# Holding back the last pair's second half in the recurrent layer's closing weave

## The chip, the cores and the metric

The kernel runs on one core of a Trainium2 chip. The metric is the device time of one execution in microseconds (us). Three executions of the kernel before the change took 1380.64, 1379.71 and 1378.60 us; the median is 1379.71 us. One further execution was recorded by the profiler, and every duration below comes from that one.

## The reference

A two-layer encoder trunk works on one sequence of 512 positions with 1024 channels. Layer 0 mixes positions with a recurrence of 12 heads (of 64 channels each) and, beside it, with attention of 4 heads into 256 memory tokens. Layer 1 uses chunked attention in place of the recurrence. Each layer ends in an output projection and a gated channel mixer. Cut to what the change touches, layer 0 is:

```
h = rms_norm(x, ln1[0]);  p = h @ a_w_in[0]
mix = rwkv7_time_mix(h, p[..., :3 * D_MIX], ...)        # the recurrence, 12 heads
mo  = memory_attention(p[..., 3 * D_MIX:], mem_n, ...)  # softmax(q k^T / 8) v, 4 heads
x = x + jnp.concatenate([mix, mo], axis=-1) @ w_out[0]

# inside rwkv7_time_mix, per head:
def step(state, inp):
    r_t, w_t, k_t, v_t, a_t, b_t = inp
    sa = jnp.einsum('bhvk,bhk->bhv', state, a_t)
    state = (state * w_t[:, :, None, :] + sa[..., None] * b_t[:, :, None, :]
             + v_t[..., None] * k_t[:, :, None, :])
    return state, jnp.einsum('bhvk,bhk->bhv', state, r_t)
# then a norm over each head's 64 channels, a bonus term, and a gate g
```

## The kernel before, in words

Everything is kept transposed, channels on the 128 partitions and the 512 positions along the free axis. A product of two fp32 operands is done as three products of a high and a low part (`r1h` and `r1l` of an activation, `whi` and `wlo` of a weight tile): `dense` writes them as pairs of matmuls on L198 and L199 for `whi`, then those on L202 for `wlo`.

The 12 heads of the recurrence go in 6 pairs, 0 to 5, and each pair goes through three generators of steps. `prepare` projects r, k and v, forms the keys, and solves a triangular system per 64-position chunk: the vector engine (DVE) works through 31 dependent rows in tile `Xs` (L661 to L668), the result goes to DRAM as `d2` and comes back as `Tt` (L671 and L674, issued on SP's queue). `front` forms products of keys and queries (`ML`, `VT`). `back` is the second half of a pair. It loads the gate's weights `g2` (L771), transposes a part of `Tt` (L775), does a chain of small matmuls (L780, L788, L794, L804, L815, L821, L830, with copies and vector operations between), then steps a state through the 8 chunks (L835 on the tensor engine PE, L836 on DVE, and the output on L840), normalises (copy L844, square L847, reduction L549, reciprocal root, transposes L558, then L856 to L858), applies the gate (L184 to L186, L867) and writes the pair's rows of `r1h` and `r1l` (L214, L215).

The order of the work is set when the program is built. `weave` takes several generators with a weight each. It keeps a clock of its own in ns, always takes a step from the one that is least far along for its weight, and adds the cost that the step yields. A step that yields `(cost, wait)` also keeps its generator from going on until the weave's clock has moved on by `wait`; a step that yields a condition keeps it until the condition holds. The tile framework then schedules the recorded instructions and gives every engine a fixed queue, worked off strictly in its order.

The last weave of layer 0 has four generators: the `back` of pair 4 (`a_`); `front` and then `back` of pair 5 (`b_`), which uses other buffers (`other_tiles`) and waits, just before its gate, for pair 4's `back` to be over; the memory's queries, reload of pairs 0 to 3 and memory attention (`q_mem`, `flush_mix`, `mA`); and `ahead`, the first two output tiles of the output projection for all inputs but pair 5's. In memory attention a score tile (L921) goes through a row maximum (L269), two exponentials (L273), a reciprocal (L275), two scalings (L278), four transposes each into two banks (L286), copies (L289) and the product with the values (L296). The small PSUM tiles `pss` of all four generators share a pool of 4 banks.

After the weave, `out_proj` finishes these two tiles with pair 5's rows and goes on with six more. The residual input `xT` (L951) is loaded into memory that the recurrent layer occupied until then.

## Time and profile before

| | |
|---|---|
| time of the profiled execution | 1377.77 us |
| its span, first to last instruction | 1376.0 us |
| median of the three timed executions | 1379.71 us |
| PE busy | 1319.7 us, 96% of the span |
| DVE busy | 826.9 us, 60% |
| scalar engine (ACT) busy | 611.6 us, 44% |
| mean granted TensorE clock | 0.987 of full speed |
| the last weave of layer 0 | about 290 to 379 us in the span |

PE is busy nearly all the time, so the profile is read by its exceptions: stretches in which PE waits, and stretches in which its clock is granted at less than full speed. A row of the timeline gives start, duration, engine, line, operation, the tiles as out<-in, and how many instructions were merged; in square brackets stands how long the engine had been idle before and who released it. In the trace one matmul of 64 or 128 columns between fp32 tiles counts twice (x32 where the program's order has x16).

### The profile page before, as it was taken

How to read it: one execution, taken by the hardware profiler on the slowest of the kernel's cores; microseconds unless marked ns; L12 is line 12 of the kernel's file. 1: busy time of each engine (PE TensorE's matmuls, PEld its weight loads, DVE VectorE, ACT ScalarE, POOL GpSimd, SP SyncE). 2: the span in 40 equal slices, each digit the busy share in tenths (PEclk: the TensorE clock that was granted, in tenths of full speed). 3: DMA queues.
4: the chain of work that ended last, by engine and by line, in shares of the span. 5: the costliest groups of instructions: out<-in, count | busy, mean ns of one | idle time of the engine just before them, and what ended most of it. 6: DMA issues, size and time to landing. Idle time of an engine off the chain costs nothing. (4 is left out here: it accounts for less than half of the span.)

```text
span 1376.0 us, 20868 instructions
## 1 busy us (share of the span) xinstructions
PE 1319.7 (96%) x8266; PEld 1071.2 (78%) x8266; DVE 826.9 (60%) x1752; ACT 611.6 (44%) x1022; POOL 34.1 (2%) x55
## 2 busy tenths in 40 slices
PE   6999999995999999999999999999999999999996
PEld 5777777774688888888888878786788888888886
DVE  7876789774666555565333667657665565563324
ACT  5556555552444333333222566657443333332321
POOL 3000000000000000000000000000000000000000
PEclk9999999997999999999999999999999999999998
DMA  5276544451042223223232422223223222222332
GB/s 181 83 208 136 109 108 110 99 142 42 24 146 92 92 94 106 92 93 102 84 98 85 152 91 74 90 92 99 93 92 103 96 93 102 98 88 85 104 94 75
DMA packets 63506, 139.18 MB, mean 101 GB/s; under 512 B 24624, under 2 KB 28336, under 8 KB 63408
## 3 DMA queue, kind: packets, MB, share of 16 engines
q1 hardware_dynamic: 60672, 127.89, 29.3%
q0 software_dynamic: 2736, 9.96, 4.2%
q8 instruction: 65, 1.06, 0.3%
q14 instruction: 33, 0.27, 0.1%
HBM read 131.01 MB, written 6.82 MB: 100 GB/s over the span
## 5 line engine op out<-in xcount | busy, mean ns | idle before, releaser
L175 DVE TENSOR_TENSOR wlo<-wraw,whi 128x1024 fp32r<-128x1024 f32 x183 | 218.9, 1197 | 128.4 <-PE psd L202 118.3
L169 ACT CAST whi<-wraw 128x1024 fp32r<-128x1024 f32 (+1 forms) x202 | 207.6, 1029 | 153.3 <-PE psd L199 38.5
L198 PE MATMUL psd<-r1h,whi 128*128 128x512 f32 x336 | 136.6, 407 | 1.3 <-ACT whi L169 1.2
L198 PE MATMUL psf<-r2h,whi 128*128 128x512 f32 x352 | 137.2, 390 | 0.0
L198 PE MATMUL psf<-r1h,whi 128*128 128x512 f32 x352 | 137.2, 390 | 0.0
L199 PE MATMUL psf<-r1l,whi 128*128 128x512 f32 x352 | 137.1, 390 | 0.0
L199 PE MATMUL psf<-r2l,whi 128*128 128x512 f32 x352 | 137.1, 390 | 0.0
L199 PE MATMUL psd<-r1l,whi 128*128 128x512 f32 x336 | 134.1, 399 | 0.0
L202 PE MATMUL psd<-r1h,wlo 128*128 128x512 f32 x336 | 92.5, 403 | 3.1 <-DMA wlo<-in_wA_dram 3.1
L199 PE MATMUL psd<-f3l,whi 128*128 128x512 f32 (+1 forms) x238 | 88.7, 377 | 0.0
L198 PE MATMUL psd<-f3h,whi 128*128 128x512 f32 (+1 forms) x238 | 88.6, 377 | 0.0
L358 DVE TENSOR_TENSOR tmp<-psf,rho 128x512 f32<-128x512 f32 x44 | 30.4, 692 | 94.7 <-PE psf L202 94.7
L202 PE MATMUL psf<-r1h,wlo 128*128 128x512 f32 x352 | 87.0, 389 | 0.0
L202 PE MATMUL psf<-r2h,wlo 128*128 128x512 f32 x352 | 86.9, 389 | 0.0
L198 PE MATMUL psd<-r2h,whi 128*128 128x512 f32 (+1 forms) x200 | 77.6, 392 | 0.1
L198 PEld LDWEIGHTS psd<-r1h,whi 128*128 128x128 f32 x336 | 63.8, 190 | 17.4 <-issue 2.4
L199 PE MATMUL psd<-r2l,whi 128*128 128x512 f32 (+1 forms) x200 | 76.4, 385 | 0.8 <-DVE r2l L215 0.8
L202 PEld LDWEIGHTS psf<-r1h,wlo 128*128 128x128 f32 x352 | 66.1, 188 | 13.7
L202 PEld LDWEIGHTS psf<-r2h,wlo 128*128 128x128 f32 x352 | 66.1, 188 | 13.7
L199 PEld LDWEIGHTS psf<-r1l,whi 128*128 128x128 f32 x352 | 66.1, 188 | 13.6
L198 PEld LDWEIGHTS psf<-r2h,whi 128*128 128x128 f32 x352 | 66.1, 188 | 13.7
L199 PEld LDWEIGHTS psf<-r2l,whi 128*128 128x128 f32 x352 | 66.1, 188 | 13.6
(352 smaller groups left out, 2429.2 us busy)
## 6 DMA issues: line engine op xcount, KB each, us to landing
wraw<-in_ffn_in_dram SPq DMA_DIRECT2D x88, 512.0 KB, 3.3
wraw<-in_ffn_out_dram SPq DMA_DIRECT2D x32, 448.0 KB, 3.3
wraw<-in_wA_dram SPq DMA_DIRECT2D x20, 512.0 KB, 4.3
wlo<-in_wA_dram POOLq DMA_DIRECT2D x17, 512.0 KB, 7.7
wraw<-in_w_out_dram SPq DMA_DIRECT2D x16, 512.0 KB, 3.8
wraw<-in_ffn_out_dram SPq DMA_DIRECT2D x16, 512.0 KB, 4.1
wraw<-in_wB_dram SPq DMA_DIRECT2D x8, 512.0 KB, 3.4
Lr<-d SPq DMA_DIRECT2D x24, 128.0 KB, 5.5
```

The source lines that it names most:

```text
L169: SC.copy(hi[:, :n], raw)
L175: V.tensor_tensor(lo[:, :n], raw, hi[:, :n], op=ALU.subtract)
L198: PE.matmul(ps, wh[:, j * P:(j + 1) * P], ah, start=start and n == 0, stop=False)
L199: PE.matmul(ps, wh[:, j * P:(j + 1) * P], al, start=False, stop=False)
L202: PE.matmul(ps, wl[:, j * P:(j + 1) * P], act(k)[0], start=False, stop=stop and n == len(ks) - 1)
L358: V.tensor_tensor(v[:], pv[:], rho[:], op=ALU.mult)
```

## The change

A new generator `later` yields one step of cost 0 and a wait of the given number of ns of the weave's clock. It is put between `front` and `back` of pair 5 with 25000 ns, so that `back` of pair 5 takes its first step only when the weave's clock has gone 25 us further. No instruction is added to or taken from the program on any engine; the queues' order changes.

```diff
+    def later(ns):
+        yield 0, ns
+
     AHEAD = [0, 1, 2, 3, 4, 6, 7]
     a_, b_ = NPAIR - 2, NPAIR - 1
     weave([(told(back(a_, Ts[a_], dst_mix), "back"), 1.5 * BACK_COST),
-           (chain(front(b_, Ts[b_]), back(b_, Ts[b_], dst_mix, other_tiles, lambda: "back" in over)),
+           (chain(front(b_, Ts[b_]), later(25000), back(b_, Ts[b_], dst_mix, other_tiles, lambda: "back" in over)),
             1.5 * (FRONT_COST + BACK_COST)),
```

What it moves shows at three places. The first is PE's queue before the change, after the second of the memory's query projections (`psd` on L202). `AR` on L780 is pair 5's transposed `Tt`, `ML` with `W` or `Tt_93` belongs to pair 4, `Tt_94` to pair 5, and `kmT` with `kn` is memory attention.

```order
L202 MATMUL psd<-r1h,wlo 128x512 x6
L830 MATMUL psl<-ML,VT 64x64 x8
L202 MATMUL psd<-r1h,wlo 128x512 x2
L780 MATMUL pss<-AR,ML 32x32
L788 MATMUL pss<-VT,ML 64x64 x12
L780 MATMUL pss<-AR,ML 32x32 x15
L788 MATMUL pss<-VT,ML 64x64 x4
L804 MATMUL pss<-VT,Tt_93 64x128 x8
L794 MATMUL pss<-Tt_94,AR 32x32 x16
```

The same place in the changed kernel's PE queue:

```order
L821 MATMUL pss<-VT,ML 64x64 x16
L198 MATMUL psd<-r1h,whi 128x512
L199 MATMUL psd<-r1l,whi 128x512
L202 MATMUL psd<-r1h,wlo 128x512 x6
L830 MATMUL psl<-ML,VT 64x64 x16
L202 MATMUL psd<-r1h,wlo 128x512 x2
L921 MATMUL pss<-kmT_85,kn 128x256 x4
L835 MATMUL psl<-W,MQ 64x64 x2
L840 MATMUL psl<-MQ,W 64x64 x2
L921 MATMUL pss<-kmT_85,kn 128x256 x4
```

Pair 5's L780 no longer follows the projection; pair 4's chain has moved ahead of it (L804, L815 and L821 stand between the projection's matmuls), and memory attention and pair 4's state steps come next.

The second place is further on in the changed kernel's PE queue, where pair 5's second half now begins. `tmp` on L549 and L558 belongs to pair 4's norm, and `kh` to the last scores of memory attention.

```order
L186 MATMUL psl<-gsh,g2l 128x512
L549 MATMUL pss<-cst,tmp 128x2 x4
L921 MATMUL pss<-kmT_85,kh 128x256 x4
L780 MATMUL pss<-AR,ML 32x32 x16
L788 MATMUL pss<-VT,ML 64x64 x16
L794 MATMUL pss<-Tt_94,AR 32x32
L184 MATMUL psl<-gsh,Xs 128x512
```

L780 of pair 5 has moved behind pair 4's state and norm and behind all eight score tiles of memory attention.

The third place is the end of the weave on PE. Before the change it reads as follows, where `psd_4632` and `psd_4661` are the output projection's first two tiles:

```order
L202 MATMUL psd_4632<-r1h_68,wlo_4628 128x512 x7
L199 MATMUL psd_4661<-r1l_69,whi_4656 128x512
L198 MATMUL psd_4661<-r1h_68,whi_4656 128x512
L199 MATMUL psd_4661<-r1l_69,whi_4656 128x512
L202 MATMUL psd_4661<-r1h_68,wlo_4657 128x512 x7
L198 MATMUL psd_4632<-r1h_68,whi_4627 128x512
L199 MATMUL psd_4632<-r1l_69,whi_4627 128x512
L202 MATMUL psd_4632<-r1h_68,wlo_4628 128x512
```

In the changed kernel these two tiles are `psd_4596` and `psd_4625`, `psd_4729` is the third, and `pss_4667` takes the transposes of pair 5's norm:

```order
L202 MATMUL psd_4625<-r1h_68,wlo_4621 128x512 x6
L558 MATMUL pss_4667<-cst_66,tmp_4665 128x128 x4
L202 MATMUL psd_4625<-r1h_68,wlo_4621 128x512
L198 MATMUL psd_4596<-r1h_68,whi_4591 128x512
L199 MATMUL psd_4596<-r1l_69,whi_4591 128x512
L202 MATMUL psd_4596<-r1h_68,wlo_4592 128x512
L198 MATMUL psd_4625<-r1h_68,whi_4620 128x512
L199 MATMUL psd_4625<-r1l_69,whi_4620 128x512
L202 MATMUL psd_4625<-r1h_68,wlo_4621 128x512
L198 MATMUL psd_4729<-r1h_68,whi_4725 128x512
```

Before, the transposes of pair 5's norm stand some forty matmuls ahead of the first that needs pair 5's rows; now only one L202 is left between them. From the third tile of the output projection on, both programs have the same order on PE.

## The prediction

> **What bounds the kernel now.** I read the page first. Its second part cuts the span into 40 slices of 34.4 us; a digit is the busy share in tenths, and PEclk the granted clock.

> ```profile
> span 1376.0 us, 20868 instructions
> ...
> PE   6999999995999999999999999999999999999996
> ...
> PEclk9999999997999999999999999999999999999998
> ```

> PE bounds the kernel everywhere but in the tenth slice (309.6 to 344 us), where it is half busy at a lower clock. That slice lies in the closing weave. Next I cut this stretch by stages; the columns are the stage, its length, then busy time on PE, PEld, DVE, ACT and POOL, granted clock and DMA.

> ```profile
> 311.70:326.40 14.70, 0.02 (x1) 0.05 (x2) 8.60 (x29) 0.81 (x2) 0.00 (x0) 0.57 0.33 75
> 326.40:340.90 14.50, 14.33 (x289) 12.95 (x289) 4.15 (x10) 5.28 (x15) 0.00 (x0) 0.84 0.03 5
> 340.90:361.70 20.80, 20.80 (x207) 13.71 (x206) 13.12 (x47) 11.11 (x34) 0.00 (x0) 1.00 0.01 2
> 361.70:380.40 18.70, 18.47 (x90) 13.91 (x89) 11.68 (x34) 8.18 (x19) 0.00 (x0) 1.00 0.24 85
> ```

> PE does nothing for 14.7 us, then is busy without a break. The timeline says who releases it, and what is done by when (PE, DVE, then SP's queue):

> ```profile
> 303.84 1.09 PE L804 MATMUL pss<-VT,Tt 64*64 64x128 f32 x16
> 310.34 0.69 PE L830 MATMUL psl<-ML,VT 128*64 128x64 f32 x16
> 310.96 0.73 PE L202 MATMUL psd<-r1h,wlo 128*128 128x512 f32 x2
> 326.38 0.28 PE L780 MATMUL pss<-AR,ML 32*32 32x32 f32 x2 [14.69 <-DVE AR L775]
> 336.58 1.15 PE L821 MATMUL pss<-VT,ML 128*64 128x64 f32 x32
> 337.66 1.96 PE L815 MATMUL pss<-ML,AR 64*64 64x128 f32 x32
> 356.58 1.05 PE L549 MATMUL pss<-cst,tmp 128*128 128x2 f32 x8
> 361.68 1.99 PE L921 MATMUL pss<-kmT,kh 64*128 64x256 f32 x8
> 378.78 0.39 PE L198 MATMUL psd<-r1h,whi 128*128 128x512 f32 x1
> 379.01 0.39 PE L199 MATMUL psd<-r1l,whi 128*128 128x512 f32 x1
> 380.41 0.50 PE L198 MATMUL psd<-r1h,whi 128*128 128x512 f32 x1
> ...
> 316.26 1.23 DVE L175 TENSOR_TENSOR wlo<-wraw,whi 128x1024 fp32r<-128x1024 f32 x1
> 319.88 0.17 DVE L668 TENSOR_TENSOR Xs<-Xs,Xu 128x8 f32<-128x8 f32 x1
> 334.94 0.42 DVE L816 TENSOR_TENSOR MQ<-pss,cst 128x256 f32<-128x256 f32 x1 [7.30 <-PE pss L815]
> 337.78 0.69 DVE L822 TENSOR_TENSOR VT<-pss,dE 128x512 f32<-128x512 f32 x1 [0.33 <-PE pss L821]
> 341.04 0.69 DVE L822 TENSOR_TENSOR VT<-pss,dE 128x512 f32<-128x512 f32 x1 [0.61 <-PE pss L821]
> 342.03 0.69 DVE L269 TENSOR_REDUCE mst<-pss 128x2 f32<-128x512 f32 x1 [0.29 <-PE pss L921]
> 369.97 0.68 DVE L856 TENSOR_TENSOR tmp<-tmp,pss 128x512 f32<-128x512 f32 x1
> 374.19 0.69 DVE L215 TENSOR_TENSOR r1l<-tmp,r1h 128x512 fp32r<-128x512 f32 x1
> ...
> 374.95 1.78 SPq L951 DMA_DIRECT2D xT<-in_xT_dram  x4
> ...
> DMA to landing us min/median/max: 3.7/5.2/6.5
> ```

> Pair 5's system is solved on DVE until 320.05 (319.88 + 0.17); the result goes through DRAM and is transposed on L775; pair 5's first matmul (326.38) waits for it, and on PE's queue pair 4's chain, ready for long, stands behind it. At the other end, pair 5's `r1l` is written at 374.88, its tiles are used at 378.78, and the output projection's third tile starts at 380.41. From there both programs have the same order on PE, so the whole effect is how much earlier, and at what clock, PE reaches that tile.

> **The change, step by step.** *The stall.* In its place come pair 4's L804 second half (1.09), L815 (1.96), L821 (1.15) and the other half of L830 (0.69). They add 4.9 to the end of the projection (311.69), less some overlap: 316.4. Then two pairs of score tiles, 1.99 each: 320.5. So the 14.7 us are covered until there.

> *DVE.* The solve is in DVE's queue ahead of the first row maximum. It now has pair 4's two L816, two L817 (0.42 each) and L822 (0.69) between its rows, 2.4 us, and loses L175 (1.23), which moves behind it. These fill gaps between dependent rows in part, so its end moves from 320.05 by 0 to 1.2; I take 320.4. Pair 4's second state step stands behind it too. PE had the result 6.3 us after the solve's end (326.38); that would now be near 327 and is hidden, since L780 comes later for another reason.

> *From the first row maximum to pair 5's L780.* ACT carries this part: two exponentials of a tile, two copies of a finished bank, one L847.

> ```profile
> 342.75 0.47 ACT L273 ACTIVATE krv<-pss,mst 128x256 f32<-128x256 f32 x1 [0.69 <-DVE mst L269]
> 343.57 0.20 ACT L273 ACTIVATION_READ_ACCUMULATOR krv<-pss,mst 128x1 f32 x1
> 349.64 1.23 ACT L289 COPY KB<-pss 128x512 f32<-128x512 f32 x2 [0.62 <-PE pss L286]
> 357.66 0.65 ACT L847 ACTIVATE tmp<-tmp 128x512 f32<-128x512 f32 x1
> ```

> A tile's exponentials take 343.77 - 342.75 = 1.02. From 320.4: row maximum 0.69, three tiles 3.1, to 324.2; the copies wait for the last transposes and end at 325.8; the fourth tile to 326.8. Only then is a bank free for the sixth score tile, which PE has after 1.0 and a state step, 328.3. Its row maximum stands on DVE behind the moved L175 (1.23), four scalings and a reciprocal: 331.2. Its exponentials and L847 end at 333.2, L549 (1.05) at 334.2, the last two score tiles (1.99) at 336.3. There L780 starts, 9.9 later than before. Bounds: the same stretch took 361.68 - 342.03 = 19.65 before with pair 5's steps in between (L780 at 342.0), and without the copies and the wait ahead of them, which hold that bank, it would be some 2 us shorter (334). The gate's weights (L771) move on SP behind the load that waits for L175; issued near 329.8 and 5 us under way as `xT` is, they come just in time.

> *Pair 5 alone.* From L780 to the end of L822 it took 341.73 - 326.38 = 15.35 with pair 4 beside it and in part at half clock; by the rows above L804 to L830 alone are 6.7 us of matmuls, with copies between that now have little to hide under. I take 11.7 with the copy behind it: 348.0. Then six state steps.

> ```profile
> 350.80 0.33 PE L835 MATMUL psd<-AR,Lr 64*64 64x64 f32 x4
> 351.18 0.28 DVE L836 SCALAR_TENSOR_TENSOR AR<-psd,dE,VT 128x64 f32<-128x64 f32 x1 [0.46 <-PE psd L835]
> ```

> One costs 0.38 + 0.28 and a hand-over, 0.7; with 3 us of transposes and value products between them, 355.1. The projection's 41 matmuls at 0.23 (378.78 to 379.01) with L549 end at 365.5, L558 at 366.1. From L856 to `r1l` it took 374.88 - 369.97 = 4.9, of which 0.5 was L857 queued on ACT: `r1l` at 370.5.

> *The end.* `xT` can only be loaded when the last tile of the recurrent layer is used, 0.07 after `r1l`, and its first quarter needs 3.7. The residual add L333 (0.69) frees the bank for the third tile. This was hidden: PE reached the third tile 5.53 after `r1l`. Now PE is early and it shows: 4.5 to 5.0 after `r1l`, so the third tile starts at 375.4 instead of 380.41. Gross gain 5.0.

> *The clock.* PE now waits about 3.5 us for pair 5's rows and, after six matmuls, 3.5 us for `xT`. What waits do to the clock:

> ```profile
> 97.60 0.73 PE L202 MATMUL psd<-r1h,wlo 128*128 128x512 f32 x2 [3.10 <-DMA wlo<-in_wA_dram]
> ...
> 98.50:99.00 0.50, 0.50 (x12) 0.50 (x12) 0.00 (x0) 0.00 (x0) 0.00 (x0) 0.86 1.03 205
> 102.00:102.50 0.50, 0.50 (x3) 0.39 (x2) 0.00 (x0) 0.00 (x0) 0.00 (x0) 0.73 1.09 254
> 313.50:314.00 0.50, 0.00 (x0) 0.00 (x0) 0.50 (x2) 0.00 (x0) 0.00 (x0) 0.90 0.25 49
> 330.50:331.00 0.50, 0.50 (x8) 0.17 (x4) 0.00 (x0) 0.02 (x1) 0.00 (x0) 0.54 0.15 33
> ```

> After 3.1 us of waiting the clock fell to half, from 98.9 to 102.3; in the long stall it fell at 313.6, and came back at 331.0, 4.6 after PE resumed. So I expect the third tile to start at half clock, 4.6 us that cost 2.3, with four chances in five: 1.8. Between 320.5 and 326.8 PE is under half busy; with one chance in two 3.4 us at half clock there cost some 1.4 on the way to L780: 0.7.

> [...]

> **Sum.** 380.41 - 375.4 = 5.0, less 1.8 and 0.7: 2.5 us earlier. The profiled execution (1376.0 span and 1.77 around it, 1377.77) would take 1375.3. It lies 1.9 below the median of the timed runs; taken from 1379.71, the forecast is 1377.2 us.

> **The rivals.**

> *The clock stays up.* The same chain without the 2.5 of clock: 1374.7. [...] Against it: the row at 97.60. Chance 0.23.

> *The held-back half starts too late (slower).* If memory attention takes as long behind the solve as before, 19.65 from the first row maximum, L780 starts at 342.0 instead of 336.3, and all behind it is 5.7 later: 5.7 - 2.5 = 3.2 slower, 1382.9. It decides from L780 at 338.8 on, where the gain is gone. For it: the same tiles share four banks, and L175 now stands among them. Against it: those 19.65 held pair 5's matmuls and state steps, which are gone from there. Chance 0.17.

> *The whole stall is won.* 14.7 and 2.3 for the half clock behind it, 17.0: 1362.7. It needs pair 5 to end with PE still busy; the 19 us of its chain between L780 and its last state step, with little beside it on PE, speak against it. Chance 0.03.

> My own case has 0.57.

> **How the numbers follow.** A measurement of this kernel can tell about 0.2%, 2.8 us, from no change. My case spreads by 2 to 2.5 around 1377.2 (the bounds of L780 and of the clock), so some two fifths of it lie below 1376.9; with the clock that stays up and the whole stall won, faster gets 0.46. Slower is the larger part of the late start, 0.13. The rest, 0.41, is within 0.2%. The range runs from 1372.9, which leaves out the whole stall and the best of the clock's case, to 1383.0, which leaves out the worst of the late start.

> **What would show it.** In the changed profile: no PE wait over 2 us between 311 and 330; L780 of pair 5 near 336; the state's last step near 355; `r1l` of pair 5 near 370.5; two PE waits of about 3.5 us ahead of the third tile, which starts near 375.4, and a granted clock of 0.5 around it. L780 at 339 or later, or `r1l` after 374, would make it wrong on one side; full clock through the third tile, or `r1l` before 368, on the other.

## The result, and the profile after

The changed kernel took 1383.82 us (median of 12 executions), the kernel before 1378.79 us beside it: ratio 1.0033, 95% interval 1.0019 to 1.0048. A second set gave 1381.89 against 1376.99 us, 1.0019 (1.0001 to 1.0036). A ratio here is that of the means, which a few quick executions lower; by medians the kernel is slower by 5 us, a third of a per cent, where 2.5 us less had been forecast. Of these 22 executions 19 took 1379.8 to 1387.2 us, with a mean granted clock of 0.979 to 0.984, and three 1370.7 to 1372.9 us, with 0.990 or 0.991. The recorded one is one of the three, so it doesn't show the loss; a usual execution, recorded later, does. The slices of the page, of the recorded execution (1370.71 us):

```profile
span 1368.9 us, 20866 instructions
PE   6999999999799999999999999999999999999996
PEclk9999999999899999999999999999999999999998
```

(The two instructions fewer than before are waits on semaphores; each engine's own work is the same.) The hole in the tenth slice and its lower clock are gone; a smaller hole, with a clock of 0.8, stands in the eleventh. The same lines of the usual execution (1381.86 us; slices of 34.5 us):

```profile
span 1380.1 us, 20866 instructions
PE   6999999999899999999999999999999999999996
PEclk9999999997889999999999999999999999999998
```

PE is as busy as in the other, but the clock is down from the tenth slice to the twelfth (310.5 to 414 us). The timeline of the recorded execution (PE, then two rows of DVE) has the forecast's stations:

```profile
300.06 1.96 PE L804 MATMUL pss<-VT,Tt 64*64 64x128 f32 x32
332.23 0.69 PE L780 MATMUL pss<-AR,ML 32*32 32x32 f32 x32
350.45 0.33 PE L840 MATMUL psd<-Lr,AR 64*64 64x64 f32 x4 [0.27 <-DVE AR L836]
365.48 0.50 PE L198 MATMUL psd<-r1h,whi 128*128 128x512 f32 x1 [3.56 <-ACT r1h L214]
371.27 0.79 PE L198 MATMUL psd<-r1h,whi 128*128 128x512 f32 x1 [2.56 <-DVE xT L333]
...
316.40 0.69 DVE L269 TENSOR_REDUCE mst<-pss 128x2 f32<-128x512 f32 x1
365.46 0.69 DVE L215 TENSOR_TENSOR r1l<-tmp,r1h 128x512 fp32r<-128x512 f32 x1 [0.69 <-ACT r1h L214]
```

And the usual execution, PE alone:

```profile
302.29 1.96 PE L804 MATMUL pss<-VT,Tt 64*64 64x128 f32 x32
320.98 0.33 PE L835 MATMUL psl<-W,MQ 64*64 64x64 f32 x4 [1.00 <-DVE W L836]
338.96 0.69 PE L780 MATMUL pss<-AR,ML 32*32 32x32 f32 x32
359.84 0.33 PE L840 MATMUL psd<-Lr,AR 64*64 64x64 f32 x4 [0.27 <-DVE AR L836]
376.50 0.50 PE L198 MATMUL psd<-r1h,whi 128*128 128x512 f32 x1 [3.56 <-ACT r1h L214]
382.12 0.80 PE L198 MATMUL psd<-r1h,whi 128*128 128x512 f32 x1 [2.57 <-DVE xT L333]
```

The waits at the end are the same in both. Executions differ by some us before the weave, so the stations are counted from the start of pair 4's L804 (303.84 before):

| us after the start of L804 | before | forecast | recorded after | usual after |
|---|---|---|---|---|
| pair 5's L780 | 22.5 | 32.5 | 32.2 | 36.7 |
| end of `r1l` of pair 5 | 71.0 | 66.7 | 66.1 | 74.9 |
| third output tile | 76.6 | 71.6 | 71.2 | 79.8 |
| from there to the end of the span | 995.6 | | 997.6 | 998.0 |

The recorded execution kept the forecast's three times within 0.6 us. The usual one reaches the third tile 79.83 - 76.57 = 3.3 us later than before and loses 2.4 behind it, 5.7 in sum; the medians say 5. Where it loses the time stands in the windows of both, the recorded one first. The columns are busy times of PE, PEld, DVE, ACT and POOL, then the granted clock:

```profile
313.80:320.70 6.90, 5.78 (x52) 4.08 (x50) 6.90 (x23) 2.84 (x12) 0.00 (x0) 1.00 0.12 19
320.70:327.60 6.90, 6.90 (x46) 3.86 (x46) 5.72 (x17) 4.38 (x13) 0.00 (x0) 1.00 0.38 101
333.10:337.70 4.60, 4.60 (x97) 3.90 (x95) 3.13 (x15) 3.81 (x12) 0.00 (x0) 1.00 0.02 5
365.90:376.30 10.40, 7.61 (x18) 5.45 (x18) 5.92 (x8) 4.47 (x6) 0.00 (x0) 0.51 0.83 302
```

The usual execution, same columns:

```profile
316.00:322.90 6.90, 5.80 (x52) 4.11 (x50) 6.90 (x23) 2.85 (x12) 0.00 (x0) 1.00 0.12 19
322.90:333.40 10.50, 10.50 (x43) 5.50 (x41) 5.77 (x17) 3.60 (x11) 0.00 (x0) 0.52 0.25 69
333.40:339.90 6.50, 6.50 (x67) 4.18 (x69) 3.48 (x13) 4.27 (x13) 0.00 (x0) 1.00 0.01 3
339.90:346.70 6.80, 6.80 (x83) 5.49 (x79) 3.11 (x14) 3.79 (x11) 0.00 (x0) 0.50 0.01 4
360.10:363.70 3.60, 3.60 (x13) 2.83 (x10) 0.00 (x0) 1.22 (x2) 0.00 (x0) 0.54 0.00 0
377.40:387.70 10.30, 7.73 (x18) 5.57 (x19) 5.66 (x7) 4.46 (x6) 0.00 (x0) 0.50 0.83 307
```

Four spells at half clock, by the half-us windows 10.2, 6.8, 3.4 and 10.2 us long, where the recorded execution has the last alone. PE is busy all through the first three. The only wait of PE close ahead of the first is the 1.00 us that ends at 320.98, and the recorded execution had that wait too (317.78 to 318.78) without a spell. No wait stands ahead of the second. Ahead of the third there are four short ones at pair 5's state steps (0.27 to 0.53 us, 1.34 in sum).

### The profile page after: what moved, and what is told of

Read it like the earlier page. It is cut to its first block, busy times and chain, and to the rows that moved or that the text cites. A ratio compares the mean times of both kernels' runs of the same rounds, so it can differ in the third digit from the quotient of the medians.

```text
span 1368.9 us, 20866 instructions
## 1 busy us (share of the span) xinstructions
PE 1319.9 (96%) x8266; PEld 1068.1 (78%) x8266; DVE 825.9 (60%) x1752; ACT 612.7 (45%) x1022; POOL 33.5 (2%) x55
## 5 line engine op out<-in xcount | busy, mean ns | idle before, releaser
L175 DVE TENSOR_TENSOR wlo<-wraw,whi 128x1024 fp32r<-128x1024 f32 x183 | 219.0, 1197 | 130.1 <-PE psd L202 118.3
L198 PE MATMUL psd<-r1h,whi 128*128 128x512 f32 x336 | 138.8, 413 | 7.3 <-ACT r1h L214 3.6
L198 PE MATMUL psf<-r1h,whi 128*128 128x512 f32 x352 | 137.1, 390 | 0.0
L198 PE MATMUL psf<-r2h,whi 128*128 128x512 f32 x352 | 137.1, 390 | 0.0
L199 PE MATMUL psf<-r1l,whi 128*128 128x512 f32 x352 | 137.0, 389 | 0.0
L199 PE MATMUL psf<-r2l,whi 128*128 128x512 f32 x352 | 137.0, 389 | 0.0
L199 PE MATMUL psd<-r1l,whi 128*128 128x512 f32 x336 | 135.7, 404 | 0.2 <-DVE r1l L215 0.2
L202 PE MATMUL psd<-r1h,wlo 128*128 128x512 f32 x336 | 92.2, 400 | 2.3 <-DMA wlo<-in_wA_dram 2.3
L199 PE MATMUL psd<-f3l,whi 128*128 128x512 f32 (+1 forms) x238 | 88.6, 377 | 0.0
L198 PE MATMUL psd<-f3h,whi 128*128 128x512 f32 (+1 forms) x238 | 88.5, 376 | 0.0
L202 PE MATMUL psf<-r1h,wlo 128*128 128x512 f32 x352 | 87.0, 389 | 0.0
L202 PE MATMUL psf<-r2h,wlo 128*128 128x512 f32 x352 | 86.9, 389 | 0.0
L198 PEld LDWEIGHTS psd<-r1h,whi 128*128 128x128 f32 x336 | 64.7, 192 | 23.9 <-ACT r1h L214 3.9
L198 PE MATMUL psd<-r2h,whi 128*128 128x512 f32 (+1 forms) x200 | 77.5, 391 | 0.1
L199 PE MATMUL psd<-r2l,whi 128*128 128x512 f32 (+1 forms) x200 | 76.3, 384 | 0.8 <-DVE r2l L215 0.8
L202 PEld LDWEIGHTS psf<-r2h,wlo 128*128 128x128 f32 x352 | 66.1, 188 | 13.8
L202 PEld LDWEIGHTS psf<-r1h,wlo 128*128 128x128 f32 x352 | 66.1, 188 | 13.8
L199 PEld LDWEIGHTS psf<-r1l,whi 128*128 128x128 f32 x352 | 66.1, 188 | 13.7
L198 PEld LDWEIGHTS psf<-r2h,whi 128*128 128x128 f32 x352 | 66.1, 188 | 13.7
L198 PEld LDWEIGHTS psf<-r1h,whi 128*128 128x128 f32 x352 | 66.1, 188 | 13.6
```

The costliest lines, as they stand in the source:

```text
L175: V.tensor_tensor(lo[:, :n], raw, hi[:, :n], op=ALU.subtract)
L198: PE.matmul(ps, wh[:, j * P:(j + 1) * P], ah, start=start and n == 0, stop=False)
L199: PE.matmul(ps, wh[:, j * P:(j + 1) * P], al, start=False, stop=False)
L202: PE.matmul(ps, wl[:, j * P:(j + 1) * P], act(k)[0], start=False, stop=stop and n == len(ks) - 1)
```

## The experiments

The theory (A): half clock makes the loss. The first expectations looked for it in the tail, that is, around the waits ahead of the third tile. After the usual execution had been recorded, A became: the clock falls where PE does small matmuls and short waits, without any long wait, and the change leaves such work alone on PE. Its rivals: pair 5's half simply starts too late (B), the loss lies in code outside the weave (C), or only waits count and additional instructions can only delay.

**The changed kernel again.** No edit.

> The changed kernel once more, to see where a usual execution spends the 13 us that the recorded one (1370.71 us) did not. Theory A, clock in the tail: the stretch from the last products with Tt of pair 4 ahead of the projection's end (L804) to the third output tile is longer than the 71.2 us of the recorded execution, or the clock stays at half for 10 us or more around and behind that tile, with the waits of 3.5 and 2.5 us as before. Theory B, late start: L780 of pair 5 comes 38 us or more after L804 (32.2 in the recorded one). Theory C, elsewhere: that stretch takes 71 to 72 us again, and the additional half clock (about 25 us of it for 12.5 us) lies ahead of 300 us or behind 380 us, in code that both kernels share. Time 1380 to 1385 for a usual execution under all three.

1381.89 us (1371.24 to 1383.33, 10 executions); the rows above are from it. L780 stands 36.7 us after L804, not the 38 of B. The spells of the weave and the tail make the difference to the recorded execution; 2.2 us more were lost ahead of the weave. C falls as the main cause, and half clock in the tail alone doesn't explain the loss either.

**The kernel before again.** No edit.

> The kernel before once more: 1376 to 1380 us, half clock near 24 to 31, 99 to 102 and 313 to 331 us. A and B expect no half clock behind 340 us; C expects that it moves between executions in code outside the weave.

1376.71 us. The half clock of the long stall lay at 315.2 to 328.9 us, 3.4 us shorter than in the first profile (313.9 to 331.0). There is none behind 340 us until the last store is awaited. Ahead of the weave the second spell lay between 110 and 120 us (113.8 to 117.2) instead of at 99 to 102, so spells do move between executions there, as C has it, but by a few us of half clock at most.

**Wide matmuls in the two waits at the end** of the changed kernel. Here and below, what stands behind a semicolon in the kernel has a line of its own where that reads better.

```diff
+    def keep(ps, n, w, x):
+        for _ in range(n): PE.matmul(ps[:], w, x, start=True, stop=True)
 # in back, behind the gate product
+        go and keep(ps_s(), 16, g2h[:], gsh[:])
 # in out_proj, ahead of the third tile
+                pre and l == 0 and m == 2 and keep(ps_s(), 16, pre[1][0][0][:, 0:P], act(0)[0])
```

> Two sets of 16 additional matmuls of 128x512 (0.23 us each, 3.7 us a set) into a bank that nobody reads stand on PE in the two waits at the end: behind pair 5's gate product, and ahead of the third output tile. The second set may delay that tile by up to 1.2 us. Theory A: no half clock from 360 to 380 us and behind it, time 1373 to 1376, ratio to before about 0.997. Theory B: as the changed kernel or up to 1 us longer, 1383 to 1385, ratio 1.003. Theory C: the same, with the half clock elsewhere.

1378.74 us, ratio to before 1.0000 (0.9984 to 1.0016), 3.2 under the changed kernel beside it. PE's timeline; L217 is the line of the additional matmuls:

```profile
371.47 3.99 PE L217 MATMUL pss<-gsh,Xs 128*128 128x512 f32 x16
377.26 3.56 PE L217 MATMUL pss<-r1h,whi 128*128 128x512 f32 x15
381.36 0.50 PE L198 MATMUL psd<-r1h,whi 128*128 128x512 f32 x1 [0.54 <-DVE xT L333]
```

The third tile starts at full clock, and from there to the end of the span it takes 996.0 us instead of 998.0, so the tail's part of A holds. The 1373 to 1376 us did not come, since spells of the weave were still there, 321.7 to 335.3 and 359.2 to 362.6 us: the tail costs some 3 us, less than the three spells (8.6, below).

**Held back by 15000 ns instead of 25000.**

> Held back by 15000 ns instead of 25000: pair 5's L780 stands behind two pairs of the first tiles of memory attention and pair 4's last state step, with half the memory attention left to lie beside pair 5's chain. L780 at about 327 (before 326.4, changed 336 by the prediction's clock). Theory A: pair 5's rows come some 5 us earlier, the wait for them is shorter and falls under memory attention's rest, less half clock in the tail, time 1370 to 1376. Theory B: the whole lateness of 9.9 us at L780 is gone, 1368 to 1374. Theory C: within 3 us of the changed kernel, 1380 to 1386.

1371.86 us (6 executions), ratio to before 0.9959 (0.9945 to 0.9973): better than both kernels. The time lies in the ranges of A and of B, so it doesn't tell them apart. The timeline and windows:

```profile
323.25 0.48 PE L835 MATMUL psl<-W,MQ 64*64 64x64 f32 x4 [1.19 <-DVE W L836]
329.46 0.31 PE L780 MATMUL pss<-AR,ML 32*32 32x32 f32 x2
374.79 0.50 PE L198 MATMUL psd<-r1h,whi 128*128 128x512 f32 x1 [0.60 <-DVE xT L333]
...
327.00:340.20 13.20, 12.75 (x135) 9.59 (x135) 1.85 (x5) 4.67 (x13) 0.00 (x0) 0.50 0.12 41
340.20:374.80 34.60, 33.81 (x294) 25.16 (x291) 19.83 (x63) 16.31 (x40) 0.00 (x0) 1.00 0.10 33
```

L780 comes 25.9 us after L804 (303.54), later than the expected 23, and the spell of 17.1 us (323.1 to 340.2) is long; but half of memory attention is left to lie beside pair 5's chain, both long waits at the end are gone, and behind 340.2 the clock is full. The third tile starts 71.3 us after L804.

**Narrow matmuls at the state steps** of the changed kernel, pairs 4 and 5, into a free column block:

```diff
-                yield 150, (600 if c < 7 else 0)
+                i > 3 and keep(psc[:, 0], 6, blk1[:], gsh[:, 0:64]); yield 150, (600 if c < 7 else 0)
```

> The changed kernel with six additional matmuls of 128x64 behind each of the seven state steps of pairs 4 and 5 (84 in all, into columns of a bank that nobody reads). A usual execution of the changed kernel is at half clock in four spells behind 320 us: 10.6, 6.8, 3.5 and 10.3 us, of which only the last follows a PE wait over 1.0 us. Theory A, the clock falls where small matmuls stand, wait or no wait: the first spell and the third (at the state steps) go, the second (at L780, no additional matmuls there) may stay, the fourth stays; 7 us less half clock or more, time 1374 to 1380, at least 2 us under the changed kernel's 1382. Rival, only waits count: the four spells stay and the additional matmuls cost 1 to 4 us, time 1383 to 1386.

1400.01 us, ratio 1.0161 (1.0147 to 1.0176). Both expectations missed: the spells neither went nor stayed, they grew together to one of 41 us. Timeline of PE, then the windows:

```profile
319.60 0.86 PE L217 MATMUL psl<-gsh,blk 128*128 128x64 f32 x6
335.38 1.47 PE L217 MATMUL psl<-gsh,blk 128*128 128x64 f32 x6
...
321.50:343.00 21.50, 21.19 (x98) 15.57 (x98) 8.19 (x27) 7.03 (x22) 0.00 (x0) 0.50 0.15 36
343.00:362.50 19.50, 19.50 (x154) 13.52 (x155) 6.78 (x25) 6.42 (x19) 0.00 (x0) 0.50 0.00 1
```

PE is busy for 40.7 of these 41 us at a clock of 0.50; its only wait, of 0.97 us, ends at 321.8. So waits are not what kept the clock down here, and matmuls of 64 columns, added as a remedy, didn't bring it back. Six take 0.86 us at full and 1.47 at half clock; by this the 84 are some 12 us of work at full clock, the larger part of the 18 us that the kernel became longer. Two more spells of 6.8 us follow (379.5 to 386.4 and 400.0 to 406.9).

**Wide matmuls at pair 4's steps** in their place:

```diff
+        kw = ps_d() if i == NPAIR - 2 else None
-                yield 150, (600 if c < 7 else 0)
+                kw and keep(kw, 2, g2h[:], gsh[:]); yield 150, (600 if c < 7 else 0)
```

> The changed kernel with two additional matmuls of 128x512 behind each of pair 4's seven state steps, in place of the narrow ones (14 of 0.23 us, 3.2 us, some 1 us of it in a wait). Theory A, the clock goes by how much of the array's time wide matmuls take and narrow ones hardly count: the long spell of the narrow version (321.5 to 362.5 us) is gone, at most one window of 3.4 us is left before 340 us, time 1376 to 1382, some 20 us under the narrow version's 1400. Rival, more instructions among the state steps hold the chain up whatever they are: 1388 to 1402, clock at half for 10 us or more from 321 us.

1375.79 us, ratio 0.9986 (0.9978 to 0.9995); 6 under the changed kernel, 24 under the narrow version, and 0.2 below the range of A. The windows:

```profile
321.50:335.50 14.00, 14.00 (x88) 9.05 (x87) 9.55 (x31) 7.04 (x23) 0.00 (x0) 1.00 0.20 55
335.50:353.00 17.50, 16.38 (x297) 12.75 (x296) 9.81 (x31) 10.49 (x27) 0.00 (x0) 1.00 0.01 2
```

The clock is full from the projection to the waits at the end. The narrow set had 84 instructions at the steps of two pairs and these are 14 at those of one; the narrow ones also write into the bank of the state steps, these into another. So the two do not differ in width alone. But it isn't PE's busy time either, since a narrow set takes longer on PE (0.86 us at full clock) than a wide one (0.73); and where the narrow version's clock fell at 321.5, with one set issued, and did not come back over all of pair 4's steps, this one's stayed up.

**Transposes as matmuls** (L286, layer 0), in the changed kernel:

```diff
-                    PE.transpose(ps[:, qt * P:(qt + 1) * P], prs[f, hh, qt // 2][:, o:o + P], C("ident"))
+                    PE.matmul(ps[:, qt * P:(qt + 1) * P], prs[f, hh, qt // 2][:, o:o + P], C("ident"), start=True, stop=True)
```

> The changed kernel with memory attention's transposes in layer 0 (L286, 32 of 128x128) written as plain matmuls with the identity instead of transposes. If transposes count for less with the clock gate than matmuls do, the first spell at half clock (322.9 to 333.4 us) goes or ends a window of 3.4 us earlier, 1.7 to 5 us less time, 1377 to 1380. If they count alike, the spells stay and the time is 1381 to 1385.

1378.34 us, ratio 1.0007 (0.9996 to 1.0017). The windows:

```profile
321.00:324.50 3.50, 3.50 (x23) 3.19 (x21) 1.75 (x7) 1.71 (x7) 0.00 (x0) 0.51 0.28 44
324.50:372.20 47.70, 42.27 (x452) 32.07 (x450) 23.12 (x71) 18.68 (x48) 0.00 (x0) 1.00 0.05 14
```

One window at half clock is left ahead of the end (3.5 us at 0.51). The result agrees with the first case of the expectation, but doesn't prove it: with the edit the scheduler also gave pair 4's state steps and the products with the values (L296) other places. And a rival stands: plain matmuls may be more work for PE. As plain matmuls each of the 32 counts twice in the trace (PE has 8298 records against 8266), so the windows hold more of them.

**Held back by 15000 ns, narrow matmuls.**

> Held back by 15000 ns, with the same 84 additional matmuls. The kernel held back by 15000 ns (1371.9 us) is at half clock from 322 to 340 us, over pair 4's state steps and pair 5's L780 to L804. Theory A: the clock stays up until pair 5's L780 at least, time 1365 to 1370. Rival, only waits count (they are 0.95 to 1.19 us there, 4.6 us in sum): half clock as before, 1372 to 1376.

1393.47 us, ratio 1.0116 (1.0097 to 1.0134). Both expectations missed: three spells, 20.5, 13.7 and 10.2 us. The narrow ones didn't keep the clock up in this order either.

**Held back by 20000 ns.**

> Held back by 20000 ns. Pair 5's L780 comes between its places with 15000 (2.9 us earlier than before, set against the end of the projection) and 25000 ns. If the order is a matter of degree, the time lies between 1371.9 and 1382 us; if the clock's spells decide, it lies near one of the two, within 2 us.

1376.06 us, ratio 0.9989 (0.9980 to 0.9998). A spell of 20.5 us and one of 3.4 at the end. The time lies between those of 15000 and 25000 ns, so it is a matter of degree.

**Held back by 15000 ns, transposes as matmuls.**

> Held back by 15000 ns, with memory attention's transposes as matmuls. In that kernel the transposes stand behind 345 us, where the clock was at full speed, and the spell (323 to 340 us) holds state steps and pair 5's chain alone. Theory A: no gain, 1370 to 1373. If plain matmuls are simply quicker than transposes, whatever the clock: 1367 to 1370.

1373.19 us, ratio 0.9971 (0.9958 to 0.9984), 0.2 above the range of A, the spell 17.1 us as before. No gain where no transposes stand in the spell (1371.86 us with them as transposes); as instructions, plain matmuls were no quicker.

**Both remedies in the changed kernel**, the transposes and the wide matmuls in the waits.

> The changed kernel (25000 ns) with both edits that took spells away: memory attention's transposes as matmuls (1378.3 us) and the 32 wide matmuls in the two waits at the end (1378.7 us). Theory A: their gains of 3.5 and 3.2 us add up, 1373 to 1377, and no spell over 3.5 us is left from 320 to 390 us. If only the phase of the clock's windows had moved in either, it stays near 1378 to 1382.

1375.52 us, ratio 0.9990 (0.9980 to 0.9999). The gains nearly add up, 6.4 us of 6.7; one window of 3.4 us is left (323.9 to 327.3).

**Held back by 15000 ns, wide matmuls at pair 4's steps.**

> Held back by 15000 ns, with the same 14 wide matmuls at pair 4's steps, where that kernel (1371.9 us) was at half clock from 323 to 340 us. Theory A: the spell shrinks to 7 us or less, 2 to 4 us gained after the matmuls' own cost, 1367 to 1371. Rival (they hold the chain up): 1373 to 1378.

1369.45 us (5 executions), ratio 0.9939 (0.9927 to 0.9951): the best of all. The timeline and windows:

```profile
302.79 1.42 PE L804 MATMUL pss<-VT,Tt 64*64 64x128 f32 x22
369.79 0.50 PE L198 MATMUL psd<-r1h,whi 128*128 128x512 f32 x1 [0.60 <-DVE xT L333]
...
327.00:340.20 13.20, 12.55 (x244) 9.98 (x245) 4.16 (x11) 6.40 (x18) 0.00 (x0) 1.00 0.09 36
340.20:369.80 29.60, 29.00 (x181) 20.72 (x180) 17.51 (x58) 14.47 (x34) 0.00 (x0) 1.00 0.11 40
```

No spell is left from 300 to 420 us. The third tile starts 67.0 us after L804, 4.3 sooner than without the additional matmuls, though these are 14 times 0.23 us of work that nobody uses.

## Why the prediction was wrong

*The stall and pair 5's chain* were right in their times. In the recorded execution, set against L804, the first row maximum came at 16.3 us (forecast 16.6), ACT's L847 ended at 29.1 (29.4), L780 came at 32.2 (32.5), the third tile at 71.2 (71.6). The gross gain was 76.57 - 71.21 = 5.4, forecast 5.0. The path to L780 was right only in part: the forecast had PE under half busy from 16.7 to 23.0 us, waiting for ACT. PE was busy for 5.2 of these 6.3 us and from there to L780 without a break, with transposes, value products and pair 4's gate product (L184 to L186). That PE's work just fitted into the time that ACT needed is luck.

*The two waits at the end* were 3.56 and 2.56 us, forecast about 3.5 each. The clock fell behind the first, 0.4 us after its end in the recorded execution (365.9) and 0.9 in the usual one (377.4), and stayed down behind the third tile's start for some 5 us, where 4.6 had been forecast (the long stall, from which the 4.6 comes, lost its clock at 313.9, not at 313.6: the row has 0.90 over half a us). That cost 2.0 and 2.4 us in the two executions; the forecast charged 1.8.

*The clock between the solve and L780* is the term that failed. The forecast saw the sparse stretch at 320.5 to 326.8 and charged 0.7: one window of 3.4 us, with one chance in two, by what waits had done to the clock before. In the usual execution there are three spells, 20.4 us, and they cost 79.83 - 71.21 = 8.6. Of this 36.67 - 32.17 = 4.5 fell on the way to L780, in place of the 0.7; the other 4.1 fell behind L780, where the forecast charged nothing until the waits at the end. The error is in what was looked for: PE waits. Busy time on PE was taken as proof of a full clock, and the three spells lie where PE is busy with score tiles, transposes, state steps, narrow products and, in the third, the first wide ones. The busy share doesn't tell the two executions apart: in the stretch of 6.90 us that ends ahead of the first spell PE was busy for 5.80 us in the usual one and for 5.78 in the same stretch of the recorded one.

*The rival of the late start* gave 1382.9 us, and the time came out near it, but not by its mechanism. L780 did pass its deciding point (338.8 by the old clock, 35.0 after L804) with 36.7. It was late because PE ran at half clock, not because score tiles waited for banks: with the same four small banks and the clock up it came 33.8 us after L804 (335.52 - 301.76, with the 14 wide matmuls). *The clock that stays up* (1374.7) describes the quick executions only in part: in the recorded one the weave's clock was up, the tail's was not. Its chance of 0.23 was the author's estimate; behind waits of 3.56 us the clock fell in both executions, for 10.2 us.

What a window held ahead of a fall can be read from the traces in part. Add up the columns of all matmul records (512 for a wide one) by the window of this grid in which each starts. The usual execution's window from 319.4 to 322.8 us has 2304 columns, and the clock fell behind it; the two in its place in the recorded execution (from 314.7 and 318.1) have 3072 and 2560, and it stayed. From 318 us on, the narrow version's window has 2176 (it fell) and that of the wide matmuls 4096 (it stayed). In the traces of the kernel before and of the recorded execution, from 30 to 1340 us, the clock fell behind the three full-clock windows with the fewest columns (512, 1792 and 2304) and behind none of the other 754, which have 2560 or more; a window full of wide matmuls has some 7700. This is a count, not a mechanism, and gives no limit: the usual execution's second spell came behind a window of some 3720 columns in which PE was busy throughout, and the count doesn't tell when the clock comes back.

## What to carry to other kernels

When a reordering fills a stall, look at what it leaves beside the chains of small matmuls elsewhere: in these runs wide matmuls put among them kept the clock up (1.00 from 321.5 to 353 us, where it was 0.50 with narrow ones). A busy share of 100% doesn't say that the clock is full (PE was busy for 40.7 of 41 us at 0.50); read the granted clock by windows of a few us wherever PE does narrow products, and in more than one execution, since a quick one may be the exception. In the windows counted here the columns started told the falls better than waits or busy time did, with the 3720 of the usual execution as the exception. Where such a chain can't be avoided, wide work beside it, even useless work, can pay (6 and 2.4 us here).

## What was not expected of the hardware

- Half clock lasted 41 us with PE busy for 40.7 of them, more than half of it matmuls of 128 columns or fewer; 84 additional matmuls of 128x64 made the kernel some 18 us longer, of which some 12 are their own time at full clock.
- Fourteen additional matmuls of 128x512 (3.2 us) made one kernel some 6 us quicker (1381.9 to 1375.8) and another 2.4 (1371.9 to 1369.5).
- The same program took 1370.7 to 1372.9 us in three executions and 1379.8 to 1387.2 us in nineteen.
